# Summing the tap products of a 31-tap convolution by accumulating DMAs in place of GpSimd adds, 13 a tile in place of 11

## The chip, the cores and the metric

The kernel runs on one core of a Trainium2 chip. The metric is the device time of one execution in microseconds. The kernel before took 3590.52 us (median of 3 runs, 3589.12 to 3595.61).

## The reference

Three transformer-like blocks run one after the other on one sequence of 1024 positions with 1024 channels, all in 32-bit floats. The change lies in the second block's convolution branch. What matters of the second block:

```
p  = rmsnorm(x, ln1_g) @ w_in
ya = rmsnorm(forgetting_attention(qa, ka, va, log_f))     # 6 heads
yb = rmsnorm(dilated_mixture(qb, kb, vb))                 # 6 heads
yc = p[gv] * sigmoid(p[gg])                               # 256 channels
yc = causal_dwconv(yc, conv_w, conv_b)                    # 31 taps, each channel by itself
yc = silu(layernorm(yc, cnorm_g, cnorm_b))
x  = x + concat(ya, yb, yc) @ w_o
# then rmsnorm, a gated feed-forward part, x + ..., rmsnorm
```

So for each of 256 channels and each of 1024 positions, the convolution sums 31 products of a weight (one for each channel and tap) and the input shifted by 0 to 30 positions, and adds a bias.

## The kernel before, in words

Activations lie with channels on the 128 partitions and positions along the free dimension. Every large matrix product is computed as three matmuls, on a high part and a remainder of both operands (whi, wlo for weights, Hh, Hl for activations): ScalarE rounds a high part (`split`, line 315), VectorE subtracts it from the source to get the remainder (line 301), and TensorE multiplies (line 320). Weights come from HBM on SyncE's (SP's) DMA queue into raw buffers. All engine operations go through small helpers, so lines 301 (two tensors), 306 (scalar, tensor, tensor), 310 (tensor and scalars), 315 and 317 (ScalarE) and 320 (matmul) occur everywhere, and a group of instructions is known by its tiles.

The program is written by Python generators. Background work such as `conv()` is a generator that is handed to `self.bg` and is resumed at each `self.step()` of the foreground, which writes the projections; each `yield` in it gives the word back. The order so written is a priority and not the last word: when the program is built, each engine gets its own fixed order, in which an instruction that is ready may stand before an earlier one that is not. Semaphore waits are put in where one instruction needs the result or the buffer of another. On the chip each engine and each DMA queue works through its own list in that order.

The convolution's 256 channels are two tiles (m = 0, 1) of 128 channels by 1024 positions. Their inputs yc are made by the projections S["g2"]. For each tile 31 taps are divided between two sums. VectorE starts ca with tap 0 and the bias (line 1546) and adds taps 13 to 30 in place, 18 instructions of one tap each (line 1551). ScalarE makes tap 1 straight into cb (line 1547) and the products of taps 2 to 12 into s, a tile with two buffers (named cs in the trace); GpSimd adds each of these 11 to cb in place (line 1555). At the end of the tile VectorE adds cb to ca (line 1560). There is one cb, so the second tile's cb is not written before this. Behind both tiles come the layer norm over the 256 channels, with matmuls against ones for the sums, a SiLU, the split, and spills to DRAM (yd).

While `conv()` is resumed, the foreground writes the value projections (vst, spilled to vd), the gate's logarithms for the first attention (`forget()`), and three pairs of query and key projections (qh, ql, spilled to qd). Then everything in the background is brought to its end (`self.drain()`, line 1692), the convolution's buffers are given back, and the attention's tables (loaded through tf) and work tiles take their memory.

The constant NP counts the taps that go to cb: 12 before, which are tap 1 and 11 more. The test in line 1553 spreads the products evenly over VectorE's taps.

Of the kernel before, what the change touches and what calls it, by code (L numbers as in the profile page):

```python
# [13 lines left out]
ALU = mybir.AluOpType  # L14
# [249 lines left out]
class Kern:  # L264
# [1244 lines left out]
    def block2(self):  # L1509
        nc, W, S, a = self.nc, self.W, self.S, self.a  # L1510
# [18 lines left out]
        cb = cp.tile([P, T], F32, name="cb")  # L1529

        def hilo():
            return [stp.tile([P, 512], F32R, tag=n, name=n) for n in ("qh", "ql")]


        NP = 12

        def conv():
            for m in range(2):
                while done[0] <= m:
                    yield  # L1540
                w = [self.col("conv_w_2", t * 2 + m) for t in range(31)]

                def mul(t, o):
                    self.act(o, yc[m][:, t:t + T], AF.Copy, scale=w[t])

                self.ts(ca[m], yc[m][:, 0:T], w[0], self.col("conv_b_2", m), ALU.mult, ALU.add)
                mul(1, cb)
                todo = list(range(2, 1 + NP))
                nd = 30 - NP
                for i, t in enumerate(range(1 + NP, 31)):  # L1550
                    self.stt(ca[m], yc[m][:, t:t + T], w[t], ca[m], ALU.mult, ALU.add)
                    if todo and (NP - 1 - len(todo)) * nd <= i * (NP - 1):
                        s = cp.tile([P, T], F32, tag="s", name="cs", bufs=2)
                        mul(todo.pop(0), s)
                        self.tt(cb, cb, s, ALU.add, nc.gpsimd)
                    if i % 3:
                        yield
                assert not todo
                yield
                self.tt(ca[m], ca[m], cb, ALU.add)  # L1560
            for _ in range(5):
                yield
            for c0, c1 in self.CH2:
                pm = self.ax()
                for m in range(2):
                    self.mm(pm, self.ones, ca[m][:, c0:c1], m == 0, m == 1)
                mu = self.tp.tile([P, 512], F32, tag="t", name="mu")
                self.act(mu, pm, AF.Copy, scale=1.0 / 256)
                ss = cp.tile([P, T], F32, tag="s", name="css", bufs=2)
                for m in range(2):  # L1570
                    x = ca[m][:, c0:c1]
                    self.tt(x, x, mu, ALU.subtract)
                    self.act(ss[:, m * 512:m * 512 + 512], x, AF.Square)
                yield
                yield
                ps = self.ax()
                self.col_sums(ps, ss[:, 0:512], ss[:, 512:T])
                r = self.var_rstd(ps[:, :4], 4, 256)
                yield
                yield  # L1580
                pb = self.ax()
                self.row_bcast(r, pb)
                for m in range(2):
                    x = ca[m][:, c0:c1]
                    self.stt(x, x, self.col("cnorm_g_2", m), pb, ALU.mult, ALU.mult)
                    self.act(x, x, AF.Silu, bias=self.col("cnorm_b_2", m))
                    hi, lo = hilo()
                    self.split(hi, lo, x)
                    self.spill(yd[0][m, :, c0:c1], hi)
                    self.spill(yd[1][m, :, c0:c1], lo)  # L1590
                yield

        done = [0]
        self.bg(conv())
        for m in range(2):
            v.memset(yc[m][:, 0:30], 0.0)
# [720 lines left out]
```

## Time and profile before

| what | value |
| --- | --- |
| median of 3 runs | 3590.52 us (3589.12 to 3595.61) |
| the profiled execution's own time | 3587.55 us |
| its span, first to last instruction | 3585.8 us |
| mean granted TensorE clock | 0.978 |
| TensorE busy | 3464.5 us (97%) |
| VectorE busy | 2249.9 us (63%) |
| ScalarE busy | 1357.7 us (38%) |
| GpSimd busy | 381.2 us (11%) |
| GpSimd's DMA queue (q0) | 5056 packets, 17.83 MB, 1.7% of 16 engines |

The profile is of one execution. Times are microseconds from the start of the span. PE is TensorE's matmuls, PEld its weight loads, DVE is VectorE, ACT ScalarE, POOL GpSimd, SP SyncE; an engine's name with a q is its sequencer or DMA queue. In a row of a group, out<-in are the program's names, x is a count, and what stands after the bars is busy time and the mean of one in nanoseconds, then the idle time before and what ended it. A busy PE is one with matmuls in flight. PEclk is the granted clock, 1.00 being 2.4 GHz and 0.50 being 1.2 GHz.

### The profile page before, as it was taken

How to read it: one execution, taken by the hardware profiler on the slowest of the kernel's cores; microseconds unless marked ns; L12 is line 12 of the kernel's file. 1: busy time of each engine (PE TensorE's matmuls, PEld its weight loads, DVE VectorE, ACT ScalarE, POOL GpSimd, SP SyncE). 2: the span in 40 equal slices, each digit the busy share in tenths (PEclk: the TensorE clock that was granted, in tenths of full speed). 3: DMA queues.
4: the chain of work that ended last, by engine and by line, in shares of the span. 5: the costliest groups of instructions: out<-in, count | busy, mean ns of one | idle time of the engine just before them, and what ended most of it. 6: DMA issues, size and time to landing. Idle time of an engine off the chain costs nothing. (4 is left out here: it accounts for less than half of the span.)

```text
span 3585.8 us, 43971 instructions
## 1 busy us (share of the span) xinstructions
PE 3464.5 (97%) x16952; PEld 2822.7 (79%) x16965; DVE 2249.9 (63%) x3605; ACT 1357.7 (38%) x2021; POOL 381.2 (11%) x368
## 2 busy tenths in 40 slices
PE   7999999999999879999999999989999999999998
PEld 7788898888887767776588788868777878877887
DVE  5456366548665793556667988776675576645444
ACT  3432254442112433555534444421242464452111
POOL 0111020000001450000021000000132320000003
PEclk9999999999999888999999999999999999999999
DMA  3111444335443126444234322254321254343222
GB/s 104 48 42 48 154 149 162 112 124 188 141 141 106 49 89 180 117 119 145 69 108 162 128 91 77 95 199 141 106 78 45 100 177 150 135 161 124 94 83 71
DMA packets 176422, 413.33 MB, mean 115 GB/s; under 512 B 17792, under 2 KB 58448, under 8 KB 176084
## 3 DMA queue, kind: packets, MB, share of 16 engines
q1 hardware_dynamic: 132852, 325.57, 28.6%
q10 hardware_dynamic: 38304, 67.13, 5.0%
q0 software_dynamic: 5056, 17.83, 1.7%
q8 instruction: 133, 2.18, 0.3%
q14 instruction: 77, 0.63, 0.1%
HBM read 304.73 MB, written 105.63 MB: 114 GB/s over the span
## 5 line engine op out<-in xcount | busy, mean ns | idle before, releaser
L320 PE MATMUL mm<-Hh,whi 128*128 128x512 f32 (+3 forms) x3632 | 1386.1, 382 | 20.8 <-DVE X L301 13.0
L320 PE MATMUL mm<-Hl,whi 128*128 128x512 f32 (+3 forms) x3632 | 1370.2, 378 | 0.0
L320 PE MATMUL mm<-Hh,wlo 128*128 128x512 f32 (+3 forms) x3632 | 1366.4, 377 | 3.0 <-DVE wlo L301 3.0
L320 PEld LDWEIGHTS mm<-Hh,whi 128*128 128x128 f32 x3632 | 687.0, 189 | 163.2 <-DVE X L301 14.4
L320 PEld LDWEIGHTS mm<-Hh,wlo 128*128 128x128 f32 x3632 | 686.1, 189 | 136.3 <-DVE wlo L301 7.0
L320 PEld LDWEIGHTS mm<-Hl,whi 128*128 128x128 f32 x3632 | 686.7, 189 | 126.5 <-issue 1.2
L315 ACT ACTIVATE whi<-raw 128x1024 fp32r<-128x1024 f32 (+3 forms) x386 | 379.1, 992 | 727.6 <-PE mm L320 485.6
L301 DVE TENSOR_TENSOR wlo<-raw,whi 128x1024 fp32r<-128x1024 f32 (+3 forms) x386 | 451.3, 1176 | 189.6 <-ACT whi L315 173.1
L301 DVE TENSOR_TENSOR X<-X,mm 128x512 f32<-128x512 f32 (+1 forms) x478 | 312.2, 657 | 393.8 <-PE mm L320 386.3
L320 PE MATMUL mm<-t,whi 128*128 128x512 f32 x1296 | 408.6, 396 | 1.5 <-ACT whi L315 1.5
L320 PEld LDWEIGHTS mm<-t,whi 128*128 128x128 f32 x1296 | 243.0, 188 | 61.4 <-ACT whi L315 2.4
L301 POOL TENSOR_TENSOR acc<-acc,sq 128x256 f32<-128x256 f32 (+1 forms) x108 | 116.1, 1076 | 1344.7 <-ACT sq L317 1341.1
L320 PE MATMUL mm<-t,wlo 128*128 128x512 f32 x648 | 256.6, 396 | 1.7 <-DVE wlo L301 1.7
L315 ACT ACTIVATE Hh<-raw 128x1024 fp32r<-128x1024 f32 x86 | 89.2, 1056 | 382.1 <-PE mm L320 227.1
L317 ACT ACTIVATE X<-X 128x512 f32<-128x512 f32 (+1 forms) x226 | 151.9, 673 | 185.5 <-DVE X L306 153.1
L301 DVE TENSOR_TENSOR raw<-raw 128x512 f32<-128x512 f32 x216 | 145.3, 688 | 78.7 <-DMA raw<-in_w_up 76.6
L320 PEld LDWEIGHTS mm<-t,wlo 128*128 128x128 f32 x648 | 121.8, 188 | 32.6 <-DVE wlo L301 3.3
L301 DVE TENSOR_TENSOR Hl<-raw,Hh 128x1024 fp32r<-128x1024 f32 x86 | 104.8, 1222 | 48.5 <-ACT Hh L315 48.0
L320 PE MATMUL mm<-wlo,Hh 128*128 128x264 f32 (+4 forms) x336 | 111.7, 341 | 12.3 <-DVE wlo L301 12.3
L306 DVE SCALAR_TENSOR_TENSOR ada<-raw,silc,ada 128x128 f32<-128x128 f32 x336 | 115.2, 350 | 7.9
L320 PE MATMUL mm<-whi,Hh 128*128 128x264 f32 (+4 forms) x336 | 111.9, 342 | 8.2 <-ACT whi L315 5.4
L1838 DVE TENSOR_REDUCE mx<-ax 128x1 f32<-128x512 f32 (+2 forms) x144 | 76.3, 554 | 61.0 <-PE ax L320 57.1
(288 smaller groups left out, 3551.2 us busy)
## 6 DMA issues: line engine op xcount, KB each, us to landing
raw<-in_w_up SPq DMA_DIRECT2D x136, 512.0 KB
raw<-gdf SPq DMA_DIRECT2D x86, 512.0 KB
raw<-in_w_down SPq DMA_DIRECT2D x86, 512.0 KB
gdf<-X ACTq DMA_DIRECT2D x108, 256.0 KB
raw<-in_w_ada SPq DMA_DIRECT2D x48, 512.0 KB
gdf<-X ACTq DMA_DIRECT2D x22, 512.0 KB
B<-qd SPq DMA_DIRECT2D x36, 256.0 KB
A<-qd SPq DMA_DIRECT2D x36, 256.0 KB
```

Source lines behind the costliest of these rows:

```text
L301: eng.tensor_tensor(out=out, in0=a, in1=b, op=op)
L306: self.nc.vector.scalar_tensor_tensor(out=out, in0=a, scalar=s, in1=b, op0=op0, op1=op1)
L315: self.nc.scalar.activation(out, in_, f, scale=scale, **kw)
L317: self.nc.scalar.activation(out, in_, f, bias=bias, scale=scale, **kw)
L320: self.nc.tensor.matmul(out, l, r, start=s, stop=e, skip_group_check=grp)
L1838: nc.vector.tensor_reduce(out=c["mx"][:, col:col + 1], in_=ps, axis=mybir.AxisListType.X, op=ALU.max)
```

## The change

ScalarE's tap products are summed into cb by DMAs that GpSimd's queue issues and that add to their destination, in place of GpSimd's own adds. NP is 14 in place of 12: ScalarE makes 13 products a tile for cb beside tap 1, and VectorE adds 16 taps in place of 18. All else is as before.

```
-        NP = 12
+        NP = 14
...
                         s = cp.tile([P, T], F32, tag="s", name="cs", bufs=2)
                         mul(todo.pop(0), s)
-                        self.tt(cb, cb, s, ALU.add, nc.gpsimd)
+                        nc.gpsimd.dma_start(out=cb, in_=s, accum_op=ALU.add)
```

## Rows read from the trace of the kernel before

**Rows 1.** The page's first part: busy time, share of the span, instructions.
```profile
span 3585.8 us, 43971 instructions
...
PE 3464.5 (97%) x16952; PEld 2822.7 (79%) x16965; DVE 2249.9 (63%) x3605; ACT 1357.7 (38%) x2021; POOL 381.2 (11%) x368
```

**Rows 2.** Busy time by stretch: length, engines (instructions), granted clock, DMA share, GB/s.
```profile
1225.00:1250.00 25.00, 19.26 (x85) 15.63 (x83) 20.52 (x10) 12.92 (x15) 16.46 (x6) 0.94 0.18 54
1250.00:1275.00 25.00, 15.19 (x75) 15.19 (x76) 24.96 (x14) 9.30 (x10) 17.95 (x6) 0.72 0.25 79
1275.00:1300.00 25.00, 21.00 (x115) 19.68 (x113) 24.86 (x23) 6.88 (x9) 10.87 (x4) 1.00 0.20 64
1300.00:1325.00 25.00, 12.75 (x37) 9.48 (x37) 24.96 (x13) 12.05 (x15) 23.81 (x8) 0.59 0.29 94
1325.00:1350.00 25.00, 23.06 (x98) 17.91 (x97) 20.75 (x21) 9.54 (x11) 0.00 (x0) 1.00 0.35 105
```

**Rows 3.** VectorE in order of time, 1225 to 1350: start, duration, operation, idle before.
```profile
1240.69 13.28 DVE L306 SCALAR_TENSOR_TENSOR ca<-yc,smalls,ca 128x1024 f32<-128x1024 f32 x4
...
1280.95 3.68 DVE L306 SCALAR_TENSOR_TENSOR ca<-yc,smalls,ca 128x1024 f32<-128x1024 f32 x3
...
1286.40 1.23 DVE L301 TENSOR_TENSOR ca<-ca,cb 128x1024 f32<-128x1024 f32 x1
...
1344.25 1.20 DVE L301 TENSOR_TENSOR ca<-ca,cb 128x1024 f32<-128x1024 f32 x1
```

**Rows 4.** GpSimd in order of time, 1225 to 1350: all there is.
```profile
1233.15 28.83 POOL L301 TENSOR_TENSOR cb<-cb,cs 128x1024 f32<-128x1024 f32 x9 [13.50 <-ACT cs L315]
1263.51 6.29 POOL L301 TENSOR_TENSOR cb<-cb,cs 128x1024 f32<-128x1024 f32 x2 [1.54 <-ACT cs L315]
1288.89 35.47 POOL L301 TENSOR_TENSOR cb<-cb,cs 128x1024 f32<-128x1024 f32 x11 [19.10 <-ACT cb L315]
```

**Rows 5.** VectorE's groups by form, 1231 to 1345.
```profile
L306 DVE SCALAR_TENSOR_TENSOR ca<-yc,smalls,ca 128x1024 f32<-128x1024 f32 x36 | 78.0, 2176 | 0.4
L301 DVE TENSOR_TENSOR wlo<-raw,whi 128x1024 fp32r<-128x1024 f32 x6 | 11.6, 1931 | 0.0
L301 DVE TENSOR_TENSOR wlo<-raw,whi 128x780 fp32r<-128x780 f32 x2 | 6.3, 3138 | 0.0
...
L301 DVE TENSOR_TENSOR yc<-yc,sgm 128x512 f32<-128x512 f32 x1 | 2.8, 2822 | 0.0
```

**Rows 6.** Waits of TensorE (1231 to 1345) and ScalarE (1200 to 1400): total, times, longest.
```profile
PE ax L1667 <- DVE zf L1633: 17.5, 3, 9.4
PE mm L320 <- DVE wlo L301: 10.2, 1, 10.2
PE mm L320 <- ACT whi L315: 5.4, 1, 5.4
...
ACT cs L315 <- POOL cb L301: 29.1, 16, 2.2
```

**Rows 7.** ScalarE in order of time, 1225 to 1350.
```profile
1230.88 1.16 ACT L315 ACTIVATE cb<-yc,smalls 128x1024 f32<-128x1024 f32 x1 [1.15 <-DVE yc L301]
...
1266.49 1.16 ACT L315 ACTIVATE cs<-yc,smalls 128x1024 f32<-128x1024 f32 x1 [1.13 <-POOL cb L301]
...
1269.83 1.15 ACT L315 ACTIVATE cs<-yc,smalls 128x1024 f32<-128x1024 f32 x1 [2.18 <-POOL cb L301]
...
1287.66 1.16 ACT L315 ACTIVATE cb<-yc,smalls 128x1024 f32<-128x1024 f32 x1 [4.56 <-DVE ca L301]
```

**Rows 8.** Busy time of two stretches, columns as in rows 2.
```profile
1231.00:1345.00 114.00, 80.26 (x362) 69.62 (x361) 113.45 (x74) 48.54 (x54) 69.09 (x22) 0.84 0.25 79
1345.00:1411.00 66.00, 61.33 (x298) 51.19 (x296) 21.47 (x44) 25.34 (x37) 0.00 (x0) 0.97 0.60 189
```

**Rows 9.** One spill of vst between VectorE and ScalarE, in order of time.
```profile
1279.17 0.55 DVE L301 TENSOR_TENSOR vst<-mm,vst 128x384 fp32r<-128x384 f32 x1
...
1282.61 0.49 ACT L315 ACTIVATE vst<-mm 128x384 fp32r<-128x384 f32 x1 [3.63 <-DMA vd<-vst]
```

**Rows 10.** GpSimd's DMAs: KB, median us to landing; then lines 959 and 1033.
```profile
X<-xd POOLq DMA_DIRECT2D x8, 1024.0 KB, 7.1
X<-sdf POOLq DMA_DIRECT2D x20, 256.0 KB, 3.7
...
DMA to landing us min/median/max: 2.8/3.6/6.7
DMA to landing us min/median/max: 5.8/7.1/10.3
```

**Rows 11.** The hand-over to the attention, in order of time: SP's queue and VectorE.
```profile
1391.01 0.32 SPq L324 DMA_DIRECT2D yd<-ql  x1
1391.43 0.69 SPq L324 DMA_DIRECT2D tf<-in_dil  x1
...
1412.45 0.29 DVE L1838 TENSOR_REDUCE mx<-ax 128x1 f32<-128x128 f32 x1 [10.70 <-PE ax L320]
```

## The prediction

> **What bounds the kernel now.** The page's first part says that TensorE is busy 97% of the span [rows 1], so a change can only pay where TensorE stands idle, and can only cost where it makes TensorE idle. The table of busy time by stretch shows where the convolution lies: between 1225 and 1350 us TensorE is busy 19.26, 15.19, 21.00, 12.75 and 23.06 us of 25, that is 33.7 us idle, and in the two worst stretches the granted clock averages 0.72 and 0.59, part of it at the lower level (1.2 GHz, 0.5), after TensorE had stood idle, while VectorE is busy 20.5 to 25.0 of 25 [rows 2]. So in this stage VectorE is the bound, not TensorE.
>
> Why VectorE is full is seen in its own order of time. A tap on it (scalar times shifted input plus sum, 128x1024) takes 1.2 us when GpSimd is idle (three in 3.68 us at 1280.95) and 3.3 us while GpSimd adds (four in 13.28 us at 1240.69) [rows 3]. GpSimd's adds run back to back, 9 in 28.83 us, 2 in 6.29, 11 in 35.47: 3.2 us each [rows 4]. The groups of the stretch 1231 to 1345 give the sum: 36 taps take 78.0 us where 36 x 1.2 = 43 would do, and the weight remainders (wlo) and yc are stretched the same way [rows 5]. The excess is 35 for the taps, some 4 for the six wide wlo, 4 for the two narrow ones and 2 for yc: about 45 us, or 2.1 us for each of the 22 adds.
>
> The waits of the stretch say what TensorE loses by it: 17.5 us on zf, 10.2 on wlo, both written by VectorE, and 5.4 on whi from ScalarE. ScalarE for its part waits 29.1 us in 16 places before a product cs until GpSimd has freed one of the two cs buffers [rows 6].
>
> **The change, part by part.** Removed: 22 GpSimd adds, and with them 45 us of stretched VectorE work; also 2 x 2 VectorE taps (4 x 1.2 = 5 us). Added: 4 products on ScalarE (4 x 1.15 = 4.6 us [rows 7]), on an engine busy 48.5 of these 114 us [rows 8], so nothing by themselves. The price is in the third part: 26 accumulating DMAs of 512 KB, 13 a tile, all into one cb. Each reads and rewrites what the last wrote, so each has to wait on GpSimd's queue until the last has landed: 13 links in a row a tile, 26 in all. The link, d, is the number that decides.
>
> Who is behind these waits? On GpSimd nobody: from 1288.89 on its work is the 11 adds, and from 1345 to 1411 it has none [rows 4, 8]. On ScalarE a product needs one of two cs buffers, so it waits for the DMA two taps earlier, and behind it stand the evacuations (vst, yc, qh) and the hi parts of weights that TensorE wants. On VectorE the sum ca+cb closes each tile and waits for the last DMA, with wlo and vst behind it. And cb of the second tile is not started before that sum: in the trace the second tile's cb comes at 1287.66, right after the sum at 1286.40 [rows 3, 7]. So the two chains don't overlap. SP's queue gets nothing new, and is passed by nothing.
>
> d from both sides. This kernel has no accumulating DMA and no SBUF-to-SBUF one. From below: the spill of vst, 384 KB from SBUF on SP's queue, is issued after VectorE ends at 1279.72, and ScalarE gets the buffer back at 1282.61: 2.9 us in all [rows 9]; 512 KB would take between that and 3.9 (scaled by size), say 3.3 us. From GpSimd's queue: 256 KB lands in 2.8 to 6.7 us, median 3.6, and 1024 KB in 5.8 to 10.3, median 7.1 [rows 10]; on the line between the medians 512 KB takes 3.6 + 3.5/3 = 4.8. An accumulate reads two operands, 1024 KB, and writes 512; so it lies between this and the 1024 KB row. From above: 10.3. I take 6.2 us, between 4.8 and 7.1 and nearer the latter, because the read side moves a full 1024 KB. It is an estimate from these rows.
>
> The Trainium skill (Collectives: The Full Stack, "The bandwidth ceiling: the fold count and why AG ≠ RS ≠ AR") says that an add in the DMA path runs at half a copy's rate, not for the add but because two sources are read; by that d would be the whole 1024 KB row, 7.1 us, and the sum below +69 us in place of +45. No run here shows an accumulate yet.
>
> **The sum.** A tile takes 1.1 us for cb's first product, 13 d, 1.2 us for the closing sum, and some 1.2 us for handovers: 13 d + 3.5. From 1230.9, where the first product stands now [rows 7], both tiles end at 1237.9 + 26 d. With d = 6.2 that is 1399; now the last closing sum ends at 1345.5 [rows 3].
>
> What hangs on this end is not lost one for one. After it come the layer norm, whose last spill is issued at 1391.01, then the load of the table tf into freed memory at 1391.43, and the attention, whose first maximum is taken at 1412.45 after VectorE waited 10.7 us [rows 11]. So the tail is 67 us now, with TensorE busy 61.3 of 66 on the projections that fill it [rows 8]. In the changed kernel much of that projection work will lie already behind TensorE, since it was free to run while ScalarE and VectorE waited (the engines' order is not the program's: two of the second tile's products, at 1266.49 and 1269.83, stand ahead of its cb [rows 7]). The norm's own chain with the hand-over I estimate at 58 us: 45 from the closing sum to the last spill less some 7 for work that no longer mixes in, and 20 from there on. Attention then starts at 1237.9 + 26 d + 58 = 1296 + 26 d instead of 1412: the change is 26 d - 116 us. It is zero at d = 4.5. With 6.2 it is +45 us.
>
> So 3587.55 (the profiled execution, span 3585.8) + 45 = 3633; the median of the three runs, 3590.52, is 3 above the profiled one, so I forecast 3635 us. The gain cannot exceed what TensorE idles in the stage, 33.7 us [rows 2], and some 5 for the lower clock (of the 12.75 us of matmuls at a mean clock of 0.59, under half would go): at best about 3549. Upper end: d = 10.3 gives +152, 3742.
>
> What is late next, once VectorE's stretched taps are gone, is the chain: VectorE's own work in the stretch falls to 113.5 - 45 - 5 = 63 us [rows 8], while the links take 26 x 6.2 = 161. The four added products on ScalarE hide in the waits of that chain; without it they would cost at most their 4.6 us. The two taps fewer a tile also take two of the twelve pauses out of the convolution's program, so it is written some four pauses earlier among the projections; I cost that at nothing, since the chain and not the place in the program ends it, and at up to four taps' time, 5 us either way, if that is wrong.
>
> **Rivals.**
> 1. *The DMAs are quick, and the kernel is faster.* If d is under 4.5 us, the chain ends before 1355, VectorE's lost 45 us come back to TensorE, and at d = 3.3 (the spill's pace) the sum is 26 x 3.3 - 116 = -30: 3561 us. For it: the spill row, which even ends in DRAM while cs and cb both lie on chip, and DMA engines only 25% busy in the stretch [rows 8, 9]. Against: the GpSimd queue's own rows are slower, and the second operand is not free. Chance 0.24. The Trainium skill (DMA: Bandwidth & Descriptors, "Anatomy of one DMA — SWDGE (gpsimd) path") gives a DMA of this queue 2.0 us plus its bytes over 436 GB/s, 3.2 us for 512 KB, and so this rival; the trace stands above the rule at both sizes it shows, 3.6 us where the rule gives 2.6 and 7.1 where it gives 4.4.
> 2. *The accumulate runs at a fraction of a copy's speed.* With d = 8 to 10.3 the sum is +92 to +152, 3683 to 3742 us. For it: the long landings of 6.7 and 10.3 when other traffic is there [rows 10], and weights and spills move here too. Against: the medians. Chance 0.16.
> 3. *The chain is hidden.* If the order that the build writes puts enough later work (second-branch values and projections) in front of the norm's matmuls, TensorE works through the chain and only a remainder shows: -10 to +20 us, 3580 to 3610. For it: the reordered products above. Against: the norm and the attention's tables stand behind the chain by memory as well, and a product waiting on ScalarE holds every evacuation after it. Chance 0.10 (0.02 faster, 0.05 no change, 0.03 slower).
>
> My forecast (d from 5 to 8: 3604 to 3682) has 0.50. Together: faster by over 0.2% 0.26, within 0.2% (7 us, about what a measurement can tell) 0.05, slower 0.69. The range 3572 to 3715 leaves out d under 3.8 and over 9.2; the forecast's own range is 3604 to 3682.
>
> **What would show it.** In the profile of the changed kernel: VectorE taps of 1.2 us throughout, none of 3.3 (if not, the first step is wrong); 26 DMAs on GpSimd's queue, each issued as the last lands, with a landing near 6 us; ScalarE's waits before cs, now 29.1 us on GpSimd, become waits on DMA of more than 60; the last ca+cb moves from 1344 to near 1398; TensorE idle and at the low clock between 1240 and 1400. The prediction is wrong in its main step if landings are below 4.5 us, or if the last ca+cb moves out and the attention's first maximum doesn't.

## The result and the profile after

The changed kernel takes 3614.56 us (median of 4 runs, 3611.48 to 3616.89), the kernel before beside it 3589.82 (4 runs): a ratio of 1.0077, 95% interval 1.0061 to 1.0092, some 25 us slower. The forecast was 45 us slower, the range 3572 to 3715. The profiled execution took 3611.48 us, 23.9 more than that of before.

The same stretches as in [rows 2] and two more, of the changed kernel: VectorE is no longer full. TensorE still idles 17.9 us between 1250 and 1325 (26.1 before), and now 34.7 us between 1350 and 1400, at a granted clock of 0.61 and 0.57.

```profile
1225.00:1250.00 25.00, 25.00 (x123) 22.31 (x122) 17.88 (x19) 12.56 (x15) 3.52 (x4) 1.00 0.63 159
1250.00:1275.00 25.00, 22.10 (x110) 21.80 (x109) 16.54 (x20) 6.94 (x9) 3.56 (x5) 0.86 0.82 187
1275.00:1300.00 25.00, 14.35 (x64) 11.85 (x63) 15.87 (x18) 10.23 (x13) 4.13 (x5) 0.80 0.77 180
1300.00:1325.00 25.00, 20.68 (x79) 15.98 (x78) 14.43 (x14) 13.58 (x15) 3.43 (x4) 0.86 0.68 171
1325.00:1350.00 25.00, 25.00 (x108) 19.92 (x107) 5.29 (x6) 8.12 (x10) 3.42 (x4) 1.00 0.76 179
1350.00:1375.00 25.00, 1.73 (x8) 1.07 (x6) 1.24 (x2) 5.22 (x5) 4.28 (x5) 0.61 0.60 128
1375.00:1400.00 25.00, 13.60 (x53) 10.59 (x54) 9.71 (x24) 10.60 (x17) 0.00 (x0) 0.57 0.16 59
```

In the kernel before, TensorE was full in the last two:

```profile
1350.00:1375.00 25.00, 25.00 (x127) 20.45 (x126) 10.82 (x22) 13.46 (x20) 0.00 (x0) 1.00 0.47 163
1375.00:1400.00 25.00, 25.00 (x125) 21.90 (x124) 9.05 (x21) 8.27 (x12) 0.00 (x0) 1.00 0.60 205
```

VectorE's taps by form and the two closing sums in order of time, against [rows 3, 5]. No tap is stretched any more; the last sum waits 12.06 us for a DMA.

```profile
L306 DVE SCALAR_TENSOR_TENSOR ca<-yc,smalls,ca x32: 1266/1280/1286, 1231.3 to 1308.4; 128x1024 f32<-128x1024 f32 x32
...
1303.04 1.23 DVE L301 TENSOR_TENSOR ca<-ca,cb 128x1024 f32<-128x1024 f32 x1 [5.91 <-DMA cb<-cs]
...
1374.72 1.22 DVE L301 TENSOR_TENSOR ca<-ca,cb 128x1024 f32<-128x1024 f32 x1 [12.06 <-DMA cb<-cs]
```

GpSimd in order of time, its 26 DMA issues (two neighbours, and the first and last of each tile), and their landing, against [rows 4, 10]. Within a tile each is issued some 5 us after the one before. The idle time in brackets is then the wait for the landing of the one before, which the profile calls issue in some rows; the first of each tile waits for ScalarE. ("To landing" counts from the start of the issue.)

```profile
1232.98 0.95 POOL L1555 DMA_DIRECT2D cb<-cs  x1 [13.72 <-ACT cs L315]
1238.02 0.87 POOL L1555 DMA_DIRECT2D cb<-cs  x1 [4.09 <-issue]
1242.92 0.85 POOL L1555 DMA_DIRECT2D cb<-cs  x1 [4.03 <-issue]
...
1295.61 0.86 POOL L1555 DMA_DIRECT2D cb<-cs  x1 [4.14 <-DMA cb<-cs]
1306.00 0.86 POOL L1555 DMA_DIRECT2D cb<-cs  x1 [9.53 <-ACT cb L315]
...
1370.32 0.86 POOL L1555 DMA_DIRECT2D cb<-cs  x1 [4.08 <-DMA cb<-cs]
...
DMA to landing us min/median/max: 4.4/4.5/7.4
```

The waits of ScalarE (1200 to 1400) and TensorE (1231 to 1445), against [rows 6]: the layer norm's first matmul waits for the chain's end, and ScalarE stands 79 us before products.

```profile
ACT cs L315 <- DMA cb<-cs: 79.1, 24, 4.8
...
PE ax L320 <- DVE ca L301: 24.3, 1, 24.3
PE ax L1667 <- DVE zf L1633: 15.0, 3, 9.6
PE mm L320 <- DVE ql L306: 11.4, 2, 7.7
```

The hand-over to the attention, VectorE in order of time, against [rows 11]: 1438.89 in place of 1412.45, 26.4 us later, about what the whole kernel is.

```profile
1438.89 5.71 DVE L1838 TENSOR_REDUCE mx<-ax 128x1 f32<-128x128 f32 x12 [5.56 <-PE ax L320]
```

### The profile page after: what moved, and what is told of

Same layout as the page of the kernel before. It is cut to its first block, busy times and chain, and to the rows that moved or that the text cites. A ratio compares the mean times of both kernels' runs of the same rounds, so it can differ in the third digit from the quotient of the medians.

```text
span 3609.7 us, 44016 instructions
## 1 busy us (share of the span) xinstructions
PE 3471.7 (96%) x16965; PEld 2828.7 (78%) x16965; DVE 2201.3 (61%) x3601; ACT 1359.8 (38%) x2023; POOL 334.7 (9%) x372
## 5 line engine op out<-in xcount | busy, mean ns | idle before, releaser
L301 DVE TENSOR_TENSOR wlo<-raw,whi 128x1024 fp32r<-128x1024 f32 (+3 forms) x386 | 441.6, 1151 | 208.0 <-ACT whi L315 190.9
L317 ACT ACTIVATE e<-ax 128x512 f32<-128x512 f32 (+2 forms) x144 | 68.2, 488 | 119.9 <-PE ax L320 118.9
```

The source lines that it names most:

```text
L301: eng.tensor_tensor(out=out, in0=a, in1=b, op=op)
L317: self.nc.scalar.activation(out, in_, f, bias=bias, scale=scale, **kw)
```

## The experiments

Ratios are against the kernel before on the same chip. The last ca+cb, the attention's first matmul (fox,identb) and ScalarE's waits before cs (1225 to 1375) come from each run's profile.

| run | adds to cb by | ratio (95%) | last ca+cb | first fox | waits before cs | landing |
| --- | --- | --- | --- | --- | --- | --- |
| before | GpSimd, 11 | 1 | 1344 | 1412 | 29.1 | |
| changed | DMA, 13 | 1.0077 (1.0061 to 1.0092) | 1375 | 1439 | 79.1 | 4.5 |
| np12dma | DMA, 11 | 1.0013 (1.0002 to 1.0023) | 1351 | 1413 | 61.2 | 4.5 |
| np14pool | GpSimd, 13 | 1.0017 (1.0008 to 1.0026) | 1339 | 1418 | 40.2 | |
| two | DMA, 12 into two sums | 0.9974 (0.9963 to 0.9986) | 1337 | 1405 | 44.3 | 6.1 |
| np8dma | DMA, 7 | 0.9945 (0.9930 to 0.9960) | 1335 | 1401 | 38.9 | 4.7 |
| dveonly | none | 0.9878 (0.9863 to 0.9893) | 1336 | 1387 | 0 | |
| unread | DMA, 13, result unread | 0.9990 (0.9979 to 1.0000) | 1316 | 1409 | 61.6 | 4.5 |
| traffic | none; 13 DMAs beside | 0.9924 (0.9906 to 0.9941) | 1344 | 1405 | 0 | 5.2 |
| np6two | DMA, 4 into two sums | 0.9893 (0.9875 to 0.9911) | 1330 | 1384 | 14.8 | 6.8 |

**The two halves of the change apart.** np12dma keeps the DMAs and takes NP back; np14pool keeps GpSimd's adds and raises NP.

```
np12dma:  NP = 12, nc.gpsimd.dma_start(out=cb, in_=s, accum_op=ALU.add)
np14pool: NP = 14, self.tt(cb, cb, s, ALU.add, nc.gpsimd)
```

> Only the way of adding is changed, the split of taps stays as before: 11 accumulating DMAs a tile, 18 taps on VectorE. Chain theory (the time is the length of the chain of links, 5.3 us from one DMA's issue to the next in the changed kernel, and the attention starts some 63 us after its end): 22 links in place of 26, so the last ca+cb near 1231 + 7 + 22 x 5.3 = 1355 us in place of 1375, and 3592 us (-21 against the changed kernel, about the kernel before). Rival, held evacuations (what costs is ScalarE standing 79 us before products while evacuations queue behind): these waits fall by 4 of 26, some 12 us of which TensorE feels a third: about 3610. Rival, traffic (the DMAs slow the weight loads and spills): bytes fall by 4 of 26, about 3610.

> The other part of the change alone: NP is 14, the sums stay on GpSimd, 13 adds a tile. GpSimd's 13 x 3.28 = 43 us a tile; VectorE loses 4 taps (-5 us) and is held by 4 more adds (+8): within 5 us of the kernel before, 3585 to 3595. Were the count the reason for the loss, it would come near 3612.

np12dma took 3592.1 us, np14pool 3593.68, with 3586.3 and 3586.41 before. Each half alone measures some 0.2% or less; the DMAs with four links more cost 0.8%. Four links at 5.3 us are 21 us; the two DMA versions differ by 0.64%, 23 us. np12dma's last sum came at 1351, where 1355 was expected. The chain theory met this; the rivals' 3610 did not.

**Shorter chains.** two has a second sum; np8dma fewer links; dveonly none.

```
two:     NP = 14
         cb = [cp.tile([P, T], F32, name="cb%d" % i) for i in range(2)]
         ...
         mul(1, cb[0]); mul(2, cb[1])          # todo from 3; at the end ca += cb[0], cb[1]
         nc.gpsimd.dma_start(out=cb[len(todo) % 2], in_=s, accum_op=ALU.add)
np8dma:  NP = 8
dveonly: NP = 1, and the lines with s (product and DMA) are gone
```

> NP stays 14, but there are two sums, cb0 and cb1, used in turn, and both are added to ca at the end: 12 DMAs a tile of the same 512 KB, two of which can be in flight. Chain theory: 6 links a tile one behind the other, each with its product 6.4 us, so a tile takes about 45 us, the last ca+cb near 1321 us, and the kernel is faster than before by 20 to 35 us: 3555 to 3570. Rival, held evacuations: ScalarE still waits for one of two cs buffers each time, waits about halve, 3595 to 3605. Rival, traffic: same bytes in less time, no better than the changed kernel, 3612 or more, with landings of 8 to 10 us in place of 4.5.

> NP is 8: 7 accumulating DMAs a tile, 22 taps on VectorE. Chain theory: 14 links, last ca+cb near 1231 + 7 + 14 x 5.3 = 1312 us unless VectorE, with 12 taps more (63 + 14 = 77 us of work), ends later, near 1315; faster than before by 20 to 35 us: 3555 to 3570. Held evacuations: waits fall to 14 of 26, about 3598. Traffic: bytes fall to 14 of 26, about 3598.

> No product goes through cs: ScalarE makes tap 1 into cb, VectorE does the other 29 taps itself; no add on GpSimd, no accumulating DMA. This is the floor of the first step (VectorE taps at 1.3 us throughout) without any link. VectorE then has 63 + 26 x 1.25 = 96 us of work from 1231 on, so the last ca+cb near 1330 us, 15 us before the kernel before: 3570 to 3580 us. If the GpSimd adds did not hold VectorE, 26 taps more on the engine that is full would make it slower than before, 3610 or more.

They took 3579.75, 3567.32 and 3545.35 us with 3586.3 before. All three end their sums at the same time, 1335 to 1337, and by the chain theory alone should be equal; they are not. two missed its 3555 to 3570 (its landing rose to 6.1 us with two DMAs in flight), and dveonly beat its 3570 to 3580 by 25 us. two's sum was expected to end near 1321 and np8dma's near 1315, so that np8dma met its time with an end 20 us off: no support for the theory. (No closing sum of np8dma waits for a DMA any more; VectorE's own list sets its end.) So the end of the sum is not all. What falls in the same order as the time is ScalarE's wait before products: 44.3, 38.9, 0. The number of DMAs, 24, 14 and 0, falls so too; the runs after these set the two apart. The stretches 1231 to 1345 of the changed kernel, of two and of dveonly, in this order, show what TensorE loses there: it is busy 96.13 and 85.33 us against 113.99 of 114, with VectorE at 66.96, 71.63 and 107.36. The changed kernel loses more behind this stretch.

```profile
1231.00:1345.00 114.00, 96.13 (x428) 82.94 (x427) 66.96 (x71) 47.89 (x55) 17.20 (x20) 0.90 0.75 180
```
```profile
1231.00:1345.00 114.00, 85.33 (x382) 72.53 (x381) 71.63 (x76) 56.14 (x62) 20.62 (x24) 0.88 0.84 196
```
```profile
1231.00:1345.00 114.00, 113.99 (x536) 97.36 (x535) 107.36 (x112) 34.05 (x47) 0.00 (x0) 1.00 0.40 132
```

dveonly's taps in this stretch, all of 1.28 us:

```profile
L306 DVE SCALAR_TENSOR_TENSOR ca<-yc,smalls,ca 128x1024 f32<-128x1024 f32 x58 | 73.7, 1278 | 0.5
```

**The chain's end and the waits apart.** In unread the chain runs into a tile cj that nothing reads, so that no sum waits for its end; in traffic it runs without products. In both, cj is first written by one more product.

```
unread:  cj = cp.tile([P, T], F32, name="cj")
         ...
         ss = cb                               # the layer norm's squares, in place of a cs buffer
         ...
         nc.gpsimd.dma_start(out=cj, in_=s, accum_op=ALU.add)
traffic: (dveonly) after every second tap, 13 a tile:
         nc.gpsimd.dma_start(out=cj, in_=yc[m][:, t:t + T], accum_op=ALU.add)
```

> As the changed kernel (13 products a tile on ScalarE, 13 accumulating DMAs into one sum, two cs buffers), but the DMAs add to a tile cj that nothing reads; ca+cb adds a cb that holds tap 1 alone, so 13 taps a tile are left out of the result. The chain and ScalarE's waits stay, only VectorE's wait for the chain's end goes (the layer norm's squares use cb, so that they don't wait for a cs buffer either). Chain theory (the end of the sum sets the start of layer norm and attention): last ca+cb near 1312 us, attention's first matmul near 1388, 3555 to 3565. Held evacuations (ScalarE standing before products holds vst, yc, qh and whi, and TensorE with them; the four runs so far have last ca+cb at 1336 to 1338 in three of them and yet 3580, 3567 and 3545 us, in the order of ScalarE's waits before products, 44, 39 and 0 us): waits still near 75 us, so 3585 to 3605.

> VectorE does all taps but one (as in dveonly, 3545 us), and beside it the 26 accumulating DMAs of 512 KB run one behind the other, from the tap's own shifted input (yc) into a tile cj that nothing reads. So the chain and its traffic are there, without products on ScalarE and without waits for cs. Held evacuations (ScalarE's waits are the second price, the one that unread still pays): within 8 us of dveonly, 3540 to 3555. Traffic (the DMAs slow weights and spills, or GpSimd's work on them holds VectorE): near unread, 3575 or more, with VectorE taps over 1.3 us or TensorE waiting on DMAs.

unread took 3581.77 us, between the two expectations: its last ca+cb came at 1316, 20 us before dveonly's, and yet it is 1.1% slower. From 1225 to 1440 its TensorE waits for zf, which VectorE copies right behind a vst that ScalarE must evacuate first, for vst itself, and for the layer norm's squares (cb), which ScalarE makes among the products; dveonly's TensorE has none of these waits.

```profile
PE ax L1670 <- DVE zf L1636: 9.5, 3, 5.5
PE ax L320 <- ACT cb L317: 7.5, 2, 4.5
PE mm L320 <- DVE zf L1636: 4.7, 2, 3.9
PE mm L320 <- ACT vst L315: 4.6, 1, 4.6
```

traffic took 3562.95, also between, and VectorE's taps in it take 1.28 us: GpSimd's DMAs do not stretch VectorE. Its ScalarE waits longer for spills: 28.7 us on vd and 15.0 on qd in 1225 to 1375, against 20.7 and 1.0 in dveonly (first rows traffic's, then dveonly's).

```profile
ACT vst L315 <- DMA vd<-vst: 28.7, 7, 7.4
ACT qh L315 <- DMA qd<-qh: 15.0, 4, 5.6
```
```profile
ACT vst L315 <- DMA vd<-vst: 20.7, 5, 5.1
...
ACT qh L315 <- DMA qd<-qh: 1.0, 1, 1.0
```

Laid one behind the other, the ratios give the steps from the changed kernel to dveonly: changed to unread 0.87%, 31 us, for VectorE and the layer norm waiting for the chain's end; unread to traffic 0.66%, 24 us, for ScalarE standing before products with the evacuations behind it; traffic to dveonly 0.46%, 16 us, for the transfers beside the spills. The pairs differ in VectorE's load and in the order of work too, and in unread and traffic the memory of cj is still held until the last DMA lands, so these are sizes and not exact shares. The first step is no clean cut either: unread's layer norm issues its last spill 67 us after its last sum (1317 to 1384), dveonly's 31 us (1337 to 1368). More cs buffers, which would let ScalarE go on while a DMA is under way, were not tried; that would be the direct test of the second step.

**What a link is made of.** copy leaves the add out, so that a tile's cb is its last product; half sends half of the positions.

```
copy: nc.gpsimd.dma_start(out=cb, in_=s)
half: nc.gpsimd.dma_start(out=cb[:, 0:512], in_=s[:, 0:512], accum_op=ALU.add)
```

> As the changed kernel, but the DMAs copy cs over cb and do not add, so each tile's cb ends as its last product alone. It measures the same link without the second operand. If the read of a second operand is the price (as the prediction had it), landing falls from 4.5 to 3.5 to 4 us, the 26 links shorten by some 20 us and the kernel is near 3595. If the add costs nothing, landing stays at 4.5 and the time at 3612.

> As the changed kernel, but each DMA adds only the first 512 of 1024 positions (256 KB; the other half of these taps is left out). It splits the link into a fixed part and a part by size. On the line of the changed kernel's rows for GpSimd's queue (256 KB 3.6, 1024 KB 7.1): landing about 3.3 us, a link of 4.1, last ca+cb near 1231 + 7 + 26 x 4.1 = 1345, about 3585. If the link were all fixed cost: landing 4.5, 3612; all size: landing 2.3, 3560.

One run each, so without an interval: copy 3578.18 us, half 3590.41, with 3586.41 before. Their landings, first copy's, then half's:

```profile
DMA to landing us min/median/max: 2.8/3.2/6.4
```
```profile
DMA to landing us min/median/max: 3.2/3.3/6.1
```

half met its expected landing, and its last sum (1346) the expected 1345. copy landed faster than the 3.5 to 4 expected. A plain 512 KB copy on chip lands in 3.2 us, the accumulate of 512 KB in 4.5, that of 256 KB in 3.3. So 256 KB of accumulate are worth 1.2 us and the fixed part is 4.5 - 2.4 = 2.1. If the copy's fixed part is the same, its own transfer is 1.1, and the accumulate's 2.4 is twice as much. That is not shown: GpSimd's issue takes 0.86 us with the add and 0.53 without, and if the copy's fixed part is less by this 0.33, the factor is 1.7.

**A try for the fastest.** np6two is two with NP = 6.

> A try for the fastest: two sums as in two, but only 4 accumulating DMAs a tile, spread over 24 VectorE taps. VectorE has 10 taps less than in dveonly (12 us), the chain of 2 links a sum is never late, ScalarE should wait little (under 10 us). If TensorE is the bound once neither VectorE, the chain nor ScalarE holds it, as dveonly's full TensorE from 1225 to 1375 says: the same as dveonly within 6 us, 3540 to 3551. If VectorE still sets dveonly's time: faster by up to 12 us, 3533.

It took 3549.28 us with 3588.88 before; the interval of its ratio overlaps dveonly's. With 48 VectorE taps in the two tiles in place of 58 it is no faster, and TensorE waits for the attention's loads (6.9 us on A<-qd), as in dveonly (6.1 on B<-qd). dveonly, 3545.35, beats both kernels, the kernel before by 1.2%, some 44 us.

## Why the prediction was right, and where it was off

**VectorE and the adds: right.** 32 taps at 1.28 us, none of 3.3; dveonly and traffic, with 58 such taps and no add on GpSimd, show it again (73.7 us in 1231 to 1345). The relief is there to be had: dveonly, without any link, is 44 us faster. That this is close to the 45 us of stretched work is chance, since its VectorE takes on 22 more taps, 28 us, in place of GpSimd's adds; what came back is TensorE's idle time, 113.99 us busy of 114 where it was 80.26 [rows 8]. The gain is above the 39 that were called the best case. That bound counted the idle time and the low clock of the stage alone; dveonly's further gain comes after it. The time from the first fox matmul to the last yT of the dilated branch is shorter, 1387 to 1774, against 1412 to 1823: 387 projection matmuls (mm) stand in it in place of 484, the others being done by then, and their busy time is 15 of these 24 us less (104.1 in place of 119.5).

**One chain that waits for itself: right.** 26 DMAs, each issued after the last had landed, the second tile's only after the first tile's sum; nobody behind them on GpSimd.

**The length of the link: mis-sized.** The term was d = 6.2; measured from issue to issue it is (1295.61 - 1232.98)/12 = 5.22 us in the first tile and (1370.32 - 1306.00)/12 = 5.36 in the second, 5.3 on the whole: landing 4.5, some 0.5 from the landing to the next issue, and now and then a landing that comes late (the longest link is 6.8). No product comes late within a tile. The estimate started from GpSimd's DMAs out of DRAM (4.8 us on the line between 256 and 1024 KB) and added for the second operand; a copy on chip takes 3.2, and the spill row, taken as the lower end at 3.3, was the nearer neighbour. That d is too high by 0.9 us costs 26 x 0.9 = 23 us, half of the forecast loss. And it could have been worse: the sum took a link for a landing, with 1.2 us a tile for hand-overs and none from one DMA to the next. With the median landing of 4.5 in it the sum gives +1 us, no loss; the oversized landing stood in for the missing hand-over and the late landings, and that the forecast still has the right sign owes something to luck. Put into the prediction's sum, 26 x 5.29 - 116 = +21.5 us, with +23.9 in the profile and +25 in the medians. The chain's end by it is 1237.9 + 137.5 = 1375.4; it was 1375.9. The tail was 63 us, not 58, which hides 5 us of the error in d.

The Trainium skill (DMA: Bandwidth & Descriptors, "Anatomy of one DMA — SWDGE (gpsimd) path") gives, as an estimate from its fixed part of 2.0 us and its rate, 3.2 us for 512 KB, and copy measures 3.2; the prediction had held the rule too low, on rows that read DRAM. The half rate for an add of the Trainium skill (Collectives: The Full Stack, "The bandwidth ceiling: the fold count and why AG ≠ RS ≠ AR") is stated there for the reduce step of a collective between cores. Carried over to the size part of this DMA it gives, as an estimate from both pages, 2.0 + 2 x 1.2 = 4.4 us; the trace has 4.5. The prediction had put it on a whole row out of DRAM and got 7.1.

**The signs: one badly set.** The prediction called itself wrong in its main step for landings below 4.5 us, and the median is just 4.5. What counts is the link, landing and hand-over together, and that is above the break-even of 4.5. The other signs came: taps of 1.28 us, waits before cs of 79.1 us, the last sum at 1375 (1398 was said), the attention moved with it. TensorE idled less widely than was said: not from 1240 on, but in part of 1250 to 1325 and in 1350 to 1400.

**That only the chain's end counts: incomplete.** It was right for this change and for np12dma, where the chain is the last to end: by the sum 22 x 5.29 - 116 = 0 us, measured +6 (ratio 1.0013). Once the chain is short or gone, as in two, np8dma and dveonly, the last sum ends at the same time in all three, and yet the kernels differ by 34 us. The prediction named the mechanism (behind a waiting product stand the evacuations) and gave it no price; unread's waits show it.

**The rivals.** Quick DMAs: the landing was nearly so, but not the link, 5.3 and not under 4.5. A fraction of a copy's speed: of the size part perhaps a half, but the link is 5.3 and not 8 to 10.3. A hidden chain: no, TensorE waited 24.3 us for the closing sum.

## What to carry to other kernels

Before work is moved off an engine, look at whether it is what makes another engine slow: here GpSimd's adds made VectorE's taps 2.6 times as long, and of the places tried the cheapest for the taps was VectorE itself. A chain of DMAs that add to one buffer costs its length times the link (landing and hand-over), and a producer that waits for it holds what stands behind it on its engine (here ScalarE, 79 us). Price the link by the nearest transfer of the same kind, on chip or out of DRAM, before the size is scaled.

## What the runs showed of the hardware

An accumulating DMA of 512 KB within SBUF lands in 4.5 us on GpSimd's queue (changed kernel, median), a plain one in 3.2 (copy), the accumulate of 256 KB in 3.3 (half); with up to two accumulates in flight the median is 6.1 (two). Chained, the next is issued 5.2 to 5.4 us after the last on average. Such DMAs leave VectorE's taps of 128x1024 at 1.28 us (changed kernel, traffic), where GpSimd's own adds beside them stretch them to 3.3 [rows 3, 4].
